# A Hymba decoder layer on one core: which modulation rows are summed in the v and z stage and which beside the xBC tiles

## The chip, the cores and the metric

The kernel runs on one core of one Trainium2 chip. The metric is device microseconds of one execution of the program; where several runs are given, their median. Engines are named as in the profile: PE is TensorE (PEld its weight loads), DVE is VectorE, ACT is ScalarE, POOL is GpSimd, SP is SyncE, which only issues DMAs here.

## The reference, cut to what matters

One sequence of 1024 tokens, width 1024, one layer:

```python
h = rmsnorm(x) * (1 + scale1) + shift1
q, k, v, z, xBC, dt = split(h @ w_in)
y_attn = rmsnorm(sliding_window_attention(q, k, v, sinks, rel_bias), attn_out_norm)
y_ssm = gated_rmsnorm(ssd_scan(silu(conv4(xBC)), dt, ...), silu(z))
x1 = x + gate1 * (concat(y_attn, y_ssm) @ w_o)
h2 = rmsnorm(x1) * (1 + scale2) + shift2
out = rmsnorm(x1 + gate2 * swiglu(h2), final_norm)
```

shift1, scale1, gate1, shift2, scale2 and gate2 are the six sections of silu(c) @ w_ada + b_ada, each of 1024 numbers, that come from the vector c of 1024 conditioning values. Attention has a window of 128, 8 query heads and a bias by relative position; everything is float32.

## The kernel before, in words

**Products.** A float32 product is made of three TensorE products in a rounded 32-bit format (`mm3`, L93): each operand is split into a high part (ACT's cast, L90) and a low part (VectorE's subtraction, `sub`, L81). A weight tile of 128x1024 is loaded by SP into `raw_ring` and split by `load_w` into `ws_ring`. `raw_ring` (L123) has three slots of 128x1024, and everything that passes through it waits for a slot to be read out.

**The six sections.** Sections 0 and 1 are computed first. Sections 2 (first gate), 3 and 4 (second norm's shift and scale) are the *rows*: `ada_row(sec, parts, kks)` (L399) loads, for each kk, one 128x1024 block of the weights through `raw_ring`, and VectorE multiplies it by one column of the conditioning and adds it to an accumulator (L407 for the first of eight, L409 for the others; `ada_rest` is `in_ada_rest` in the trace). The accumulator still has to be summed over its 128 partitions. For the gate, `gate` (L411) does it with two products against a matrix of ones (psg, L414), after its bias row has been loaded through the ring and added (L420 to L422). For the second norm, `second_mod` (L637) makes sixteen transposes into four psum banks (ps_gv, L642) and four reductions on VectorE (L643).

**Stages around the change.** The v and z projection runs over eight tiles of 128 tokens (`vz_tile`), each with two of the four psum banks of tag mm (vza and vzb). ACT frees them with a copy and two tanh, VectorE with two products (L369) and an addition. After tile 3 the bias table is built: a product, VectorE's L390, and three ACT DMAs gd (L392), gr (L394, one row copied to all partitions of a DRAM buffer, 1.5 MB) and tb (L396). Then come the gate's rows (`ada_row(2, ...)`, L419), the first three xBC weights (L423), the tiles 4 to 7 and `gate`. Next, four attention tiles `attn(t)` (L443) and the eight xBC tiles of half 0 (`xbc_tile`, L502). One attention tile is: scores (pss, L459), VectorE's bias and maximum (L463, reads tb), ACT's exponentials (L469), transposes (pst, L479), the product with v (psy, L486), VectorE's scaling (`mul`, L84), ACT's square sum, rstd over VectorE (L145), GpSimd (L146) and ACT, ACT's scaling (L492), and the four transposes of `mix_out` (psm_a, L438), whose split is one more L81. One xBC tile is 24 products psx of 128x512 and, on VectorE, three conv products (L515) and a gating one. The rows of sections 3 and 4 stand behind the xBC tiles, by the numbers of `MOD_ROWS`; `second_mod` follows them, and then the scan (`ssd_prep` with pacs, L554, and the operand w2, L564; `ssd_chunk` with seg, L581).

**What sets the order.** The program text is not the order of an engine: when the program is built, a scheduler puts each engine's instructions into a fixed order, in which psx products fill in between the steps of attention. SP's loads keep the program's order (L72). Each engine and each queue then works in order, and an instruction that has to wait holds up what stands behind it. The psum tag sm also has four banks, shared by all small products (pss, pst, psy, psm, psg, ps_gv, seg).

## Time and profile before

| | |
|---|---|
| median of 3 runs | 1148.93 us (1146.12 to 1150.82) |
| profiled execution | 1144.76 us, span 1143.0 us |
| mean granted clock of TensorE | 0.987 |
| busy in the span | PE 1105.0 (97%), PEld 912.4 (80%), DVE 842.6 (74%), ACT 517.2 (45%), POOL 244.6 (21%) |
| DMA | 197.29 MB, mean 173 GB/s |
| v and z tiles 0 to 7 on PE | end at 153.26 us |
| first xBC tiles and attention of tiles 0 to 3 | 156 to 240 us |

The times of the trace are those of one profiled execution, counted from the start of its span. Busy times are sums over instructions of an engine; PE's are modelled ends of pipelined products, so PE busy isn't PE at its peak. A row of the timeline gives start, duration, line, operation and, in brackets, how long the engine stood idle before it and what released it. The granted clock is a share of 2.4 GHz.

### The profile page before, as it was taken

How to read it: one execution, taken by the hardware profiler on the slowest of the kernel's cores; microseconds unless marked ns; L12 is line 12 of the kernel's file. 1: busy time of each engine (PE TensorE's matmuls, PEld its weight loads, DVE VectorE, ACT ScalarE, POOL GpSimd, SP SyncE). 2: the span in 40 equal slices, each digit the busy share in tenths (PEclk: the TensorE clock that was granted, in tenths of full speed). 3: DMA queues.
4: the chain of work that ended last, by engine and by line, in shares of the span. 5: the costliest groups of instructions: out<-in, count | busy, mean ns of one | idle time of the engine just before them, and what ended most of it. 6: DMA issues, size and time to landing. Idle time of an engine off the chain costs nothing. (4 is left out here: it accounts for less than half of the span.)

```text
span 1143.0 us, 15497 instructions
## 1 busy us (share of the span) xinstructions
PE 1105.0 (97%) x5376; PEld 912.4 (80%) x5376; DVE 842.6 (74%) x1490; ACT 517.2 (45%) x1007; POOL 244.6 (21%) x185
## 2 busy tenths in 40 slices
PE   7999999999999889999999999999999999999996
PEld 6788987787788668887888888888888878888875
DVE  6895368788856466546888888898788648787856
ACT  4573256756565456535443333333333325555431
POOL 0100000001200111000222124554445010451352
PEclk9999999999999969999999999999999999999998
DMA  7555644421320253236753247556764468788733
GB/s 267 189 173 174 238 151 145 137 74 38 148 75 19 102 185 119 76 127 221 249 189 125 67 148 263 194 179 217 256 201 160 157 226 306 252 292 281 234 104 147
DMA packets 80449, 197.29 MB, mean 173 GB/s; under 512 B 9154, under 2 KB 10226, under 8 KB 80244
## 3 DMA queue, kind: packets, MB, share of 16 engines
q1 hardware_dynamic: 74164, 184.95, 47.4%
q10 hardware_dynamic: 6208, 11.37, 2.8%
q8 instruction: 42, 0.69, 0.2%
q14 instruction: 35, 0.29, 0.1%
HBM read 149.87 MB, written 47.98 MB: 173 GB/s over the span
## 5 line engine op out<-in xcount | busy, mean ns | idle before, releaser
L81 DVE TENSOR_TENSOR FR<-FP,FR 128x512 fp32r<-128x512 f32 (+4 forms) x244 | 195.0, 822 | 68.8 <-ACT FR L90 68.3
L90 ACT CAST FR<-FP 128x512 fp32r<-128x512 f32 (+3 forms) x236 | 157.7, 682 | 185.6 <-PE psg L95 79.8
L797 POOL TENSOR_TENSOR GF<-GF 128x512 f32<-128x512 f32 x77 | 124.0, 1633 | 68.9 <-DMA GF<-in_w_dn 65.8
L94 PE MATMUL psg<-FR 128*128 128x512 f32 x306 | 119.0, 389 | 0.0
L95 PE MATMUL psg<-FR 128*128 128x512 f32 x306 | 119.0, 389 | 0.0
L96 PE MATMUL psg<-FR 128*128 128x512 f32 x306 | 119.0, 389 | 0.0
L146 POOL TENSOR_TENSOR FP<-FP 128x1 f32<-128x1 f32 (+1 forms) x40 | 28.3, 713 | 407.8 <-DVE FP L145 351.6
L87 DVE TENSOR_TENSOR GF<-GF,psg 128x512 f32<-128x512 f32 x126 | 84.2, 680 | 30.4 <-PE psg L96 27.9
L90 ACT CAST FR<-GF 128x512 fp32r<-128x512 f32 x77 | 47.4, 619 | 79.8 <-PE psg L95 54.5
L94 PE MATMUL psg<-GR,FR 128*128 128x512 f32 x198 | 77.0, 389 | 0.0
L95 PE MATMUL psg<-GR,FR 128*128 128x512 f32 x198 | 77.0, 389 | 0.0
L96 PE MATMUL psg<-GR,FR 128*128 128x512 f32 x198 | 77.0, 389 | 0.0
L81 DVE TENSOR_TENSOR FR<-GF,FR 128x512 fp32r<-128x512 f32 x77 | 73.1, 951 | 0.9 <-ACT FR L90 0.7
L95 PEld LDWEIGHTS psg<-FR 128*128 128x128 f32 x306 | 57.4, 188 | 12.0
L94 PEld LDWEIGHTS psg<-FR 128*128 128x128 f32 x306 | 57.4, 188 | 11.9
L96 PEld LDWEIGHTS psg<-FR 128*128 128x128 f32 x306 | 57.4, 188 | 11.9
L803 POOL TENSOR_TENSOR GD<-GD 128x512 f32<-128x512 f32 x23 | 35.7, 1562 | 119.7 <-ACT GD L415 57.7
L800 POOL TENSOR_TENSOR GF<-GF 128x512 f32<-128x512 f32 x11 | 15.5, 1405 | 194.3 <-DVE GF L84 156.2
L94 PE MATMUL psgu<-FR 128*128 128x512 f32 x128 | 51.6, 407 | 2.5 <-DVE FR L179 1.3
L94 PE MATMUL psx<-FR 128*128 128x512 f32 x128 | 52.2, 408 | 0.0
L96 PE MATMUL psgu<-FR 128*128 128x512 f32 x128 | 51.4, 403 | 0.5 <-DVE FR L81 0.5
L95 PE MATMUL psx<-FR 128*128 128x512 f32 x128 | 51.8, 405 | 0.0
(318 smaller groups left out, 2748.6 us busy)
## 6 DMA issues: line engine op xcount, KB each, us to landing
FP<-in_w_gu SPq DMA_DIRECT2D x52, 512.0 KB, 4.2
FP<-in_ada_rest SPq DMA_DIRECT2D x24, 512.0 KB, 4.4
actds<-GF SPq DMA_DIRECT2D x44, 256.0 KB, 2.7
GF<-in_w_dn SPq DMA_DIRECT2D x22, 512.0 KB, 4.6
wdndt<-GF SPq DMA_DIRECT2D x44, 256.0 KB, 4.4
FP<-actds SPq DMA_DIRECT2D x44, 256.0 KB, 4.4
FP<-wdndt SPq DMA_DIRECT2D x44, 256.0 KB, 4.4
FP<-actda SPq DMA_DIRECT2D x33, 256.0 KB, 4.2
```

The source lines that it names most:

```text
L81: nc.vector.tensor_tensor(out=out, in0=a, in1=b, op=ALU.subtract)
L87: nc.vector.tensor_tensor(out=out, in0=a, in1=b, op=ALU.add)
L90: nc.scalar.copy(h, raw)
L94: nc.tensor.matmul(ps, lhsT=lh, rhs=rh, start=first, stop=False)
L95: nc.tensor.matmul(ps, lhsT=lh, rhs=rl, start=False, stop=False)
L96: nc.tensor.matmul(ps, lhsT=ll, rhs=rh, start=False, stop=last)
L146: nc.gpsimd.tensor_tensor(out=r, in0=r, in1=mhalf[:, 0:count], op=ALU.pow)
L797: nc.gpsimd.tensor_tensor(out=out, in0=a, in1=b, op=ALU.subtract)
L800: nc.gpsimd.tensor_tensor(out=out, in0=a, in1=b, op=ALU.add)
L803: nc.gpsimd.tensor_tensor(out=out, in0=a, in1=b, op=ALU.mult)
```

## The change

The rows of sections 3 and 4 are loaded and multiplied where those of section 2 stood, and the other way round. Section 3 stands ahead of the first three xBC weights; in the text of the program two rows of section 4 follow each of the tiles 4 to 7; the transposes and reductions of the second norm stand behind tile 7, where the gate's products were. One row of the gate follows each xBC tile of half 0, and its bias row and its products stand behind the eighth. Section 3, until now accumulated as one 128x1024, becomes two parts of 128x512, as section 4 was; section 2 remains one 128x1024. Rows, transposes, reductions and gate products are the same in number.

```diff
--- before.py
+++ after.py
@@ -18,7 +18,6 @@
 KT = 8
 NF = 22
 XNB = ((0, 4, 36, 40), (0, 4, 36, 40))
-MOD_ROWS = (3, 3, 3, 3, 2, 2, 0, 0)
 NP = 11
 WARM = (16, 5)
 EPS = 1e-6
@@ -414,16 +413,23 @@
             nc.tensor.matmul(ps, lhsT=ones, rhs=a[:, 512 * e:512 * e + 512], start=True, stop=True)
             nc.scalar.copy(g[e], ps)
 
-    arow = view(FA, 16, [D])
     gate1 = [view(FA, 14, [512]), view(FA, 48, [512])]
-    ada_row(2, [arow])
-    brow = raw_ring([D])[0:1]
-    dma(brow, adab_g[0:1])
-    add(arow[0:1], arow[0:1], brow)
+    mod2 = [[view(FA, 20 + 4 * j + 2 * k, [512]) for k in range(2)] for j in range(2)]
+    ada_row(3, mod2[0])
     xw = [load_w(w_xbc[f], [KT, P]) for f in range(3)]
     for t in range(4, 8):
         vz_tile(t)
-    gate(2, gate1, arow)
+        ada_row(4, mod2[1], [2 * t - 8, 2 * t - 7])
+    sh2, g2 = M(8), M(8)
+    gv2 = M(16)
+    for j in range(4):
+        ps = sm_bank(f"ps_gv2{j}")
+        for k in range(4):
+            nc.tensor.transpose(ps[:, k * P:(k + 1) * P], mod2[j // 2][j % 2][:, k * P:(k + 1) * P], ident)
+        nc.vector.reduce_sum(out=gv2[:, 4 * j:4 * j + 4], in_=ps.rearrange("p (a b) -> p a b", a=4), axis=AX.X)
+    add(sh2, gv2[:, 0:8], pt[:, C_ADAB + 24:C_ADAB + 32])
+    mul(g2, gv2[:, 8:16], pt[:, C_N2:C_N2 + 8])
+    add(g2, g2, nb2)
 
 
     p_w.__exit__(None, None, None)
@@ -632,29 +638,16 @@
             nc.scalar.activation(y[:, 256 * g:256 * g + 256], y[:, 256 * g:256 * g + 256], AF.Copy, scale=r[:, g:g + 1])
         mix_out(y, t, 1, f"s{t}")
 
-    sh2, g2 = M(8), M(8)
-
-    def second_mod():
-        gv2 = M(16)
-        for j in range(4):
-            ps = sm_bank(f"ps_gv2{j}")
-            for k in range(4):
-                nc.tensor.transpose(ps[:, k * P:(k + 1) * P], mod2[j // 2][j % 2][:, k * P:(k + 1) * P], ident)
-            nc.vector.reduce_sum(out=gv2[:, 4 * j:4 * j + 4], in_=ps.rearrange("p (a b) -> p a b", a=4), axis=AX.X)
-        add(sh2, gv2[:, 0:8], pt[:, C_ADAB + 24:C_ADAB + 32])
-        mul(g2, gv2[:, 8:16], pt[:, C_N2:C_N2 + 8])
-        add(g2, g2, nb2)
-
-    mod2 = [[view(FB, 18, [512]), view(FB, 20, [512])], [view(FB, 22, [512]), view(FA, 46, [512])]]
     for t in range(4):
         attn(t)
-    rows = [(3 + r // 8, r % 8) for r in range(16)]
+    arow = view(FB, 18, [D])
     for f in range(8):
         xbc_tile(0, f)
-        for _ in range(MOD_ROWS[f]):
-            sec, kk = rows.pop(0)
-            ada_row(sec, [view(FB, 18, [D])] if sec == 3 else mod2[1], [kk])
-    second_mod()
+        ada_row(2, [arow], [f])
+    brow = raw_ring([D])[0:1]
+    dma(brow, adab_g[0:1])
+    add(arow[0:1], arow[0:1], brow)
+    gate(2, gate1, arow)
     prep = ssd_prep(0)
     for t in range(4):
         ssd_chunk(t, prep)
```

**Where the scheduler puts it.** The change is written as moved code, and the order of the engines moves with it. Below, FA, FB, FP and FR are SBUF tensors, names with a number are psum banks, and the lines of the changed kernel are one less than before up to its L415 (L369 is now L368, L409 L408) and six more in attention and the xBC tiles (L459 is now L465, L515 L521). On SP the bias row of the gate moves from ahead of the first three xBC weights to behind the last row, so those three weights come one place earlier.

VectorE in the v and z stage, from the first product that frees a bank of tile 3 to the first that frees one of tile 4. vza_1077 and vzb_1078 are the banks of tile 3 in both kernels; vza_1172 (before) and vza_1178 (now) is the first bank of tile 4, which tile 6 takes again. Before:

```order
L369 SCALAR_TENSOR_TENSOR FA<-FA,vza_1077 128x196
L369 SCALAR_TENSOR_TENSOR FA<-FA,vzb_1078 128x316
L87 TENSOR_TENSOR FP<-vzb_1078,FP 128x8
L390 SCALAR_TENSOR_TENSOR FA<-ps_rel,FA 8x384
L507 COPY FA<-FP 128x3
L369 SCALAR_TENSOR_TENSOR FA<-FA,vza_1172 128x196
```

Now:

```order
L406 TENSOR_SCALAR FA<-FP 128x512 x2
L408 SCALAR_TENSOR_TENSOR FA<-FP,FA 128x512
L368 SCALAR_TENSOR_TENSOR FA<-FA,vza_1077 128x196
L408 SCALAR_TENSOR_TENSOR FA<-FP,FA 128x512 x4
L368 SCALAR_TENSOR_TENSOR FA<-FA,vzb_1078 128x316
L86 TENSOR_TENSOR FP<-vzb_1078,FP 128x8
L389 SCALAR_TENSOR_TENSOR FA<-ps_rel,FA 8x384
L408 SCALAR_TENSOR_TENSOR FA<-FP,FA 128x512 x5
L513 COPY FA<-FP 128x3
L408 SCALAR_TENSOR_TENSOR FA<-FP,FA 128x512 x4
L368 SCALAR_TENSOR_TENSOR FA<-FA,vza_1178 128x196
```

The sixteen products of section 4's eight rows (L406 and L408) now stand ahead of tile 4's first product, three of them ahead of tile 3's first and seven ahead of the mask's L390 (now L389).

TensorE right behind v and z tile 7, before:

```order
L414 MATMUL psg_0_1400<-FA,FP 128x512
L414 MATMUL psg_1_1403<-FA,FP 128x512
L459 MATMUL pss_0_1412<-FA 128x128 x2
L459 MATMUL pss_1_1417<-FA 128x128 x2
L459 MATMUL pss_2_1422<-FA 128x128 x2
L459 MATMUL pss_3_1427<-FA 128x128 x2
L94 MATMUL psx_0_1736<-FR 128x512
```

Now:

```order
L428 MATMUL ps_gv_1430<-FP,FA 128x128 x4
L428 MATMUL ps_gv_1436<-FP,FA 128x128 x4
L428 MATMUL ps_gv_1442<-FP,FA 128x128 x4
L428 MATMUL ps_gv_1448<-FP,FA 128x128 x4
L465 MATMUL pss_0_1463<-FA 128x128 x2
L93 MATMUL psx_0_1787<-FR 128x512
L465 MATMUL pss_1_1468<-FA 128x128 x2
L94 MATMUL psx_0_1787<-FR 128x512
L465 MATMUL pss_2_1473<-FA 128x128 x2
L95 MATMUL psx_0_1787<-FR 128x512
```

Sixteen transposes into four banks stand where the gate's two banks were filled, and the four pss, which came one behind the other, have one psx between each other.

VectorE in attn(0), from ahead of the product that reads psy to the rstd and behind it, before:

```order
L409 SCALAR_TENSOR_TENSOR FB<-FP,FB 128x1024
L84 TENSOR_TENSOR FA<-psy_1457,FP 128x512
L510 COPY FP<-FA 128x3
L515 SCALAR_TENSOR_TENSOR FA<-FA,FP 128x512
L409 SCALAR_TENSOR_TENSOR FB<-FP,FB 128x1024
L145 TENSOR_SCALAR FP<-FP 128x1
L515 SCALAR_TENSOR_TENSOR FA<-FA,FP 128x512
L409 SCALAR_TENSOR_TENSOR FB<-FP,FB 128x1024
L515 SCALAR_TENSOR_TENSOR FA<-FA,FP 128x512
```

Now:

```order
L477 RECIPROCAL FP<-FP 128x8
L516 COPY FP<-FA 128x3
L408 SCALAR_TENSOR_TENSOR FB<-FP,FB 128x1024
L83 TENSOR_TENSOR FA<-psy_1508,FP 128x512
L521 SCALAR_TENSOR_TENSOR FA<-FA,FP 128x512
L80 TENSOR_TENSOR FR<-FP,FR 128x1024
L521 SCALAR_TENSOR_TENSOR FA<-FA,FP 128x512
L144 TENSOR_SCALAR FP<-FP 128x1
L86 TENSOR_TENSOR FB<-FB 128x32
```

Between psy's product and L145 (now L144) a row product (L409) and a conv product stood; now two conv products and a weight split (L80, the former L81) stand there. On TensorE 22, 17, 14 and 17 psx stood between the last psy product and psm_a of attn(0) to attn(3); now it is 26, 22, 18 and 16. Between pss and the first pst there were 15 and 13 in the first two tiles, and there are 18 and 15 now.

## Rows read from the trace of the kernel before

**Rows 1.** Busy time by stretch: us, PE, PEld, DVE, ACT, POOL, PEclk, DMA share, GB/s.
```profile
156.00:180.00 24.00, 22.62 (x122) 17.45 (x121) 21.64 (x68) 18.69 (x48) 0.99 (x1) 1.00 0.52 165
180.00:200.00 20.00, 18.31 (x108) 14.75 (x108) 17.86 (x48) 10.81 (x30) 0.99 (x1) 1.00 0.51 174
200.00:220.00 20.00, 18.46 (x110) 15.08 (x109) 16.07 (x48) 13.97 (x36) 1.46 (x1) 1.00 0.33 117
220.00:240.00 20.00, 19.30 (x120) 16.65 (x119) 14.89 (x28) 13.47 (x28) 1.46 (x1) 1.00 0.41 132
```

**Rows 2.** Waits of PE from 156 to 240 us: total, times, longest.
```profile
PE psm_a L438 <- ACT FA L492: 3.4, 4, 1.1
PE pst L479 <- ACT FB L469: 1.1, 2, 0.8
PE pss L459 <- DVE FR L81: 0.8, 2, 0.4
```

**Rows 3.** Timeline of DVE, attn(0): start, us, line, operation [idle before].
```profile
165.08 1.28 DVE L409 SCALAR_TENSOR_TENSOR FB<-FP,FB 128x1024 f32<-128x1024 f32 x1 [1.18 <-DMA FP<-in_ada_rest]
...
166.28 0.68 DVE L84 TENSOR_TENSOR FA<-psy,FP 128x512 f32<-128x512 f32 x1
...
167.61 1.28 DVE L409 SCALAR_TENSOR_TENSOR FB<-FP,FB 128x1024 f32<-128x1024 f32 x1
...
168.81 0.15 DVE L145 TENSOR_SCALAR FP<-FP 128x1 f32<-128x1 f32 x1
```

**Rows 4.** Timeline of PE in the same place.
```profile
169.13 0.39 PE L94 MATMUL psx<-FR 128*128 128x512 f32 x1
169.36 0.39 PE L95 MATMUL psx<-FR 128*128 128x512 f32 x1
170.83 0.66 PE L438 MATMUL psm_a<-FP,FA 128*128 128x128 f32 x4 [1.08 <-ACT FA L492]
```

**Rows 5.** DVE by line and shape, 80 to 330 us: busy, mean ns, idle before.
```profile
L81 DVE TENSOR_TENSOR FR<-FP,FR 128x1024 fp32r<-128x1024 f32 x16 | 19.4, 1216 | 4.4 <-ACT FR L90 4.4
...
L409 DVE SCALAR_TENSOR_TENSOR FA<-FP,FA 128x1024 f32<-128x1024 f32 x7 | 9.0, 1283 | 3.1 <-DMA FP<-in_ada_rest 2.8
...
L409 DVE SCALAR_TENSOR_TENSOR FB<-FP,FB 128x512 f32<-128x512 f32 x7 | 5.2, 744 | 1.5 <-DMA FP<-in_ada_rest 1.5
...
L643 DVE TENSOR_REDUCE FP<-ps_gv 128x4 f32<-128x512 f32 x4 | 2.6, 682 | 0.0
```

**Rows 6.** DMA issues (98 to 114 us, 111 to 126 us: median to landing) and SP's timeline.
```profile
FP<-in_ada_rest SPq DMA_DIRECT2D x6, 512.0 KB, 4.8
...
FP<-in_w_xbc SPq DMA_DIRECT2D x3, 512.0 KB, 5.4
...
112.39 3.24 SPq L72 DMA_DIRECT2D FP<-in_w_xbc  x3
```

**Rows 7.** Timeline of PE: v and z tile 6 begins; the gate's products.
```profile
138.99 0.32 PE L94 MATMUL vza<-FR 128*128 128x324 f32 x1
...
153.26 1.88 PE L414 MATMUL psg<-FA,FP 128*128 128x512 f32 x4
```

**Rows 8.** Mask of the bias table: DVE's row, ACT's two issues, DMA landing.
```profile
125.00 0.54 DVE L390 SCALAR_TENSOR_TENSOR FA<-ps_rel,FA 8x384 f32<-8x384 f32 x1
...
127.21 0.56 ACTq L394 DMA_DIRECT2D gr<-gd  x1
...
135.72 0.43 ACTq L396 DMA_DIRECT2D FA<-gr  x1
...
FA<-gr ACTq DMA_DIRECT2D x1, 1024.0 KB, 8.0
```

**Rows 9.** Timelines of PE and DVE behind the last xBC tile of half 0.
```profile
240.10 0.38 PE L554 MATMUL pacs<-FP,FB 128*128 128x128 f32 x2
...
248.69 1.22 DVE L84 TENSOR_TENSOR FR<-FB,FP 128x1024 fp32r<-128x1024 f32 x1
```

**Rows 10.** Busy time by stretch, second norm of half 0 (columns as in group 1).
```profile
400.00:420.00 20.00, 16.60 (x60) 12.58 (x61) 14.59 (x25) 11.50 (x17) 2.91 (x2) 0.59 0.46 172
```

## The prediction

> **What bounds the kernel now.** I read the busy times by stretch first. From 156 to 240 us, while the first four attention tiles and the xBC tiles of half 0 run, TensorE is busy 22.62, 18.31, 18.46 and 19.30 us of 84, so 5.3 us are idle there, and VectorE is nearly full in the first half of it: 21.64 of 24 us, then 17.86 of 20 [rows 1]. Second, TensorE's waits of that stretch: 3.4 us in four waits of psm_a (the transposes of the normed attention output) for ACT's L492, 1.1 us of pst for the exponentials, 0.8 us of pss for VectorE's L81 [rows 2]. They add up to the 5.3 us, so this is all that the stage can give. Third, the timelines around psm_a of attn(0), to see who is late behind ACT. VectorE stands in a row product (L409) until 166.28, 1.18 us of it waiting for the row's transfer, and only then multiplies psy; another row product of 1.28 us stands between that and the L145 that the rstd needs [rows 3]. psm_a comes at 170.83, two us after L145, and TensorE has waited 1.08 us for it [rows 4]. So the rows lengthen the chain from psy to psm_a.
>
> **What the change removes from VectorE there.** The second norm's sixteen rows were 7 products of 128x1024 at 1.28 us, 14 of 128x512 at 0.744 us [rows 5], and three first products that I count at the same prices, which is an upper bound: 8 x 1.28 + 16 x 0.744 = 22.1 us. The first gate's eight rows come instead: 8 x 1.28 = 10.3 us. VectorE loses about 12 us of 70.5 busy in the stretch [rows 1], and about half of the head-of-line waits for landings. The four reductions (0.682 us each [rows 5]) leave the end of the stretch for its beginning.
>
> **What becomes of the waits.** TensorE's order is fixed when the program is built, and it changes with the rows. Between psy and psm_a stood 22, 17, 14 and 17 psx products; now 26, 22, 18 and 16. One psx starts 0.23 us after the other [rows 4], so the covers are 6.0, 5.1, 4.1 and 3.7 us instead of 5.1, 3.9, 3.2 and 3.9. The new chain in attn(0): the psy product 0.68 us [rows 3]; then two conv products of 128x512 (the same kind and size as the 0.744 us row) and one weight split of 1.216 us [rows 5], 2.7 us; L145 0.15 us; and the 2.0 us from L145 to psm_a [rows 3, 4]. That is 5.5 us against a cover of 6.0. The wait of 1.08 us goes, with half a us to spare. In the next two tiles the cover grows by 1.2 and 0.9 us and row products leave the chain, in the last it shrinks by one psx while VectorE is freer. I leave 0.3 us of the 3.4. The cover between pss and pst grows from 15 to 18 and from 13 to 15 psx, which is 0.5 to 0.7 us against waits of at most 0.8: I leave none of the 1.1. The pss wait needs a psum bank that VectorE's split of psm_a gives back; it is not shortened, and I keep its 0.8. **Recovered: 5.3 - 1.1 = 4.2 us.** The ends: 5.3 if all go, 1.1 if only pst's go.
>
> **What it adds to the v and z stage.** Section 3's rows take the gate's place ahead of the weights; eight more, section 4's, run beside tiles 3 and 4, where VectorE's own work is light, but it works in order, and the two psum banks of tile 4 are freed by products (L369) that now stand behind all eight rows. Tile 6 takes these banks at 138.99 [rows 7]. When are the rows done? The raw ring has three slots. The first weight load behind the rows of section 3 is issued at 112.39 now; it moves one ring slot forward, because the bias row leaves the ring, so I take about 111.5, plus 5.4 us to landing [rows 6], plus a split of about 2.3 us (ACT's cast and the 1.216 us of rows 5): the first row's load goes out near 119, the next two near 121 and 122. A slot then turns round in 4.8 us of landing [rows 6], 1.5 us for two products and 0.3 us of handing over, 6.6 us. Row 6 is issued near 132, row 7 near 134: the last product ends at 138.5 to 140.5. Tile 6 waits nothing to 2 us; I take **+0.8 us**. The upper bound comes from the gr copy below, the slowest load of this place: at its 8.5 us for the last two rows they end near 143, and tile 6 waits 4 us.
>
> Behind these rows on VectorE stands the mask's product (L390), now at 125.00; four and a half us later it starts the gd, gr and tb copies on ACT's queue. gr is issued at 127.21 and has landed by 135.72, when tb is issued; tb takes 8.0 us [rows 8]. Moved to 132, that makes 140.5 and 149, ahead of the first bias product, by my estimate near 157 (the stretch of attn(0) starts at 156): nothing, though 8 us of slack are left where there were 12. ACT's next copy, of tile 5's bank, stands behind tb's issue on its queue, some 4 us ahead of tile 7, which takes that bank: nothing.
>
> **Behind the v and z stage** sixteen transposes take the place of the gate's products, 1.88 us [rows 7]. psm_a's four transposes of the same size take 0.66 us together [rows 4], so sixteen take some 2.6 us at most, and less back to back; the same exchange the other way round stands behind the xBC tiles, so the two cancel. But they use all four small psum banks, and pss can begin in each only when its reduction is done. The reductions start when VectorE has finished tile 7, by my estimate a little over 1 us behind tile 7's end at 153.26, and follow each other every 0.68 us [rows 5, 7]; TensorE would be there some 2 us behind that end and now has a psx between the pss. I take **+0.4 us**; the ends are nothing and 2.7 us, four reductions in a row.
>
> **Behind the xBC tiles** the gate's products stand where the transposes stood; their rows were complete two tiles earlier, so they wait for none. Without the reductions the seg products move nearer to pacs: 25 psx behind it, 5.7 us, where pacs is at 240.10 and the operand's product (L84) runs from 248.69 [rows 9], 44 psx behind. VectorE has to do one split, three conv products and that one in between, 1.2 + 2.2 + 1.2 us and small ones; it is nearly even. I take **+0.4 us**, from nothing to 1. DMA traffic, ACT's work, SP's number of loads (24 rows, one bias row) and the order behind the second norm are the same; the out projection has long had its gate. GpSimd's work is the same too.
>
> **Sum.** -4.2 + 0.8 + 0.4 + 0.4 = -2.6 us. The profiled execution took 1144.76 us, so 1142.2; it lies 4.2 us under the median of the three runs, 1148.93, and against that the forecast is **1146.3 us**. From 1143.2 to 1154.7, 0.5% either way, a measurement of this kernel can't tell it from no change.
>
> **Rivals.** *The waits stay where they are.* psm_a waits for ACT and GpSimd, and the conv products and splits that are left on VectorE fill the place of the rows: the chain of attn(0) came out only 0.5 us under its cover. If it is 0.5 to 1 us longer in each tile, only pst's 1.1 us come back, and with the 1.6 us added the time is 1149.4. For it: rstd's way over three engines is not touched. Against it: in the second and third tile the cover grows by more than the chain.
>
> *The rows jam the v and z stage* (the slower side). The rows' transfers fall together with the 1.5 MB gr copy, which now starts later, beside the last rows. If each of these takes gr's 8.5 us, tile 6 waits 4 us; gr itself, at twice its 8.5 us, lands at 149, so ACT stands at tb's issue until then, frees tile 5's bank 3 us after tile 7 wants it near 146, halfway between the two rows of TensorE [rows 7], and tb lands at 157, just as the bias products ask for it. Counted 4 + 1 + 0.5 us beyond what is saved or hidden, against 4.2 - 0.8 us of gain, the time is about 1151; if the attention waits stay too, 1155. It decides from a row landing above about 6 us. In the trace one row beside gr landed in less than the 4.8 us of the others, which speaks against it. The Trainium skill (DMA: Bandwidth & Descriptors, Queues, rings and completion order) says that each DMA engine takes the queues it has work for in turn, packet by packet, so that loads of SP and copies of ACT share it. By that rule gr is drawn out by the rows for as long as rows are waiting, which is this rival's price; no run here shows the two with more than three rows.
>
> *The half-clock stretch moves.* From 400 to 420 us the granted clock is 0.59 of 2.4 GHz, so most of it is at 1.2 GHz, with 16.60 us of work [rows 10], behind the wait of the second norm's transposes for VectorE. At 2.4 GHz the work would have taken 0.59 of that, 6.8 us less. The order there is unchanged, but everything arrives earlier; if the stretch were shorter by two thirds, the time is about 1142, and a longer one costs as much as 3 us. Nothing in the change speaks for either.
>
> **How the numbers follow.** The forecast has 0.55, the staying waits 0.22, the jam 0.12, a shorter clock stretch 0.11. Faster by over 0.5% needs all 5.3 us and more, or the clock: 0.10 from the last rival and 0.07 from the forecast's edge, 0.17. Slower by over 0.5% is the worse half of the jam, 0.06, and 0.02 for what I overlook, 0.08. The rest, 0.75, is no change. The bounds of the forecast's own terms reach from 1143.6 (5.3 recovered, nothing added) to 1151 (1.1 and half of the upper bounds); the range takes in most of the clock rival at its lower end and the milder jam at its upper: 1141.5 to 1151.5.
>
> **What would show it.** Right: VectorE's busy time from 156 to 200 us falls by 8 us or more, psm_a's four waits by 2.5 us or more, the vza products of tile 6 wait under 2 us, pss waits under 1 us behind the v and z stage, and the first xBC tile of half 1 begins 2 to 4 us earlier. Wrong: psm_a still waits 3 us in all; a wait of vza above 3 us for L369; tb landing behind the first bias product; a stretch of 1.2 GHz in the v and z stage, or none near 400 us.

## The result, and the profile after

Eight runs of the changed kernel took 1155.69 us in the median (1151.26 to 1163.61), eight of the kernel before 1148.57 us (1145.71 to 1151.1): a ratio of 1.0073, with a 95% interval of 1.0053 to 1.0092. The change makes the kernel slower by 0.7%. The forecast was 1146.3 us, no change, with a range of 1141.5 to 1151.5. The profiled execution took 1155.87 us, its span 1154.1 us; the mean granted clock is 0.983 (0.987 before), PE is busy for 1111.4 us, DVE for 841.5. A *hole* below is time in which TensorE stands idle ahead of a product.

Busy time by stretch in the changed kernel, the columns and stretches of [rows 1]:

```profile
156.00:180.00 24.00, 23.21 (x109) 18.13 (x108) 16.52 (x51) 11.60 (x33) 1.20 (x1) 0.86 0.41 131
180.00:200.00 20.00, 19.73 (x115) 16.28 (x115) 16.14 (x50) 14.55 (x36) 1.46 (x1) 1.00 0.20 68
200.00:220.00 20.00, 19.79 (x115) 16.06 (x113) 16.60 (x46) 14.44 (x34) 1.54 (x1) 1.00 0.22 80
220.00:240.00 20.00, 18.19 (x108) 15.08 (x108) 13.61 (x39) 13.32 (x33) 1.69 (x2) 1.00 0.30 106
```

TensorE idles 3.1 us of the 84 where it idled 5.3, and VectorE has lost 7.6 us. But in the first stretch the granted clock is 0.86: TensorE is busy because its products take longer. Waits of PE from 156 to 242.5 us, to be held against [rows 2]:

```profile
PE psm_a L444 <- ACT FA L498: 2.4, 2, 1.5
PE pss L465 <- DVE FP L429: 0.8, 1, 0.8
PE pss L465 <- DVE FR L80: 0.7, 2, 0.4
```

Of psm_a's 3.4 us 2.4 are left, pst's 1.1 us are gone, and the scores have a new wait of 0.8 us for the reductions (L429). TensorE's timeline from v and z tile 6 to the second xBC products ([rows 7] before):

```profile
141.03 0.41 PE L93 MATMUL vza<-FR 128*128 128x324 f32 x1 [2.05 <-DVE FA L368]
...
155.39 1.91 PE L428 MATMUL ps_gv<-FP,FA 128*128 128x128 f32 x16
158.09 0.71 PE L465 MATMUL pss<-FA 64*128 64x128 f32 x4 [0.79 <-DVE FP L429]
158.73 0.50 PE L93 MATMUL psx<-FR 128*128 128x512 f32 x1
159.16 0.71 PE L465 MATMUL pss<-FA 64*128 64x128 f32 x4
159.80 0.56 PE L94 MATMUL psx<-FR 128*128 128x512 f32 x1
160.28 1.22 PE L465 MATMUL pss<-FA 64*128 64x128 f32 x4
161.44 0.79 PE L95 MATMUL psx<-FR 128*128 128x512 f32 x1
162.16 1.22 PE L465 MATMUL pss<-FA 64*128 64x128 f32 x4
```

Four things stand there that the kernel before doesn't have: 2.05 us of waiting ahead of tile 6, 0.79 us ahead of the scores, scores pulled apart by single psx, and from 160 us on everything at half speed (four scores 1.22 us where they took 0.71). The clock by stretch says the same:

```profile
158.00:162.00 4.00, 3.91 (x15) 2.62 (x15) 3.60 (x18) 0.00 (x0) 0.00 (x0) 0.76 0.40 136
162.00:166.00 4.00, 4.00 (x11) 3.08 (x11) 2.76 (x11) 1.18 (x7) 0.00 (x0) 0.50 0.05 8
```

In the kernel before, the scores of attn(0) ran as one block:

```profile
155.06 1.46 PE L459 MATMUL pss<-FA 64*128 64x128 f32 x16
156.45 0.50 PE L94 MATMUL psx<-FR 128*128 128x512 f32 x1
```

Sixteen records in 1.39 us there, four in 0.64 us here (each of the eight float32 score products leaves two records). Why the wait of the scores: the rows hold VectorE's mask product (L390, now L389), and that holds three ACT copies. DVE, then ACT's queue, in the changed kernel ([rows 8] before):

```profile
130.66 0.53 DVE L389 SCALAR_TENSOR_TENSOR FA<-ps_rel,FA 8x384 f32<-8x384 f32 x1
```

```profile
135.00 0.56 ACTq L393 DMA_DIRECT2D gr<-gd  x1
...
145.57 0.42 ACTq L395 DMA_DIRECT2D FA<-gr  x1
146.04 0.27 ACT L362 COPY FA<-vza 128x128 f32<-128x128 f32 x1 [9.77 <-DMA gr<-gd]
...
155.60 0.33 ACTq L622 DMA_DIRECT2D FA<-gzd  x1
155.97 0.27 ACT L362 COPY FA<-vza 128x128 f32<-128x128 f32 x1 [7.03 <-DMA gzd<-FA]
```

gr is issued 7.8 us later than before and takes 10.5 us to land where it took 8.5; ACT stands idle until 145.57, then frees tile 5's bank and stores two tiles shortly after each other; at 155.60 it issues the scan's first reload of the gated z (L622), which had to wait for one of these stores, and only then frees tile 7's banks, 6 us later than before. The reductions come behind that.

How much of this is the clock can be counted over all runs, since each lists its mean granted clock. I call (1 - clock) x time the *clock loss* and clock x time the *rest*. Means: before 1131.1 + 16.3 us (35 runs, beside the first experiments), changed 1136.1 + 20.1 us (8 runs). So the change costs 5.0 us of rest and 3.8 us of clock (standard errors near 0.8 and 1.4 us). The eight runs of the kernel before that stand beside the changed ones have no clock on record; their mean is 1148.4 us, 1.0 us above those 35, so up to 1 us of these 8.8 can be a difference between the two sets of runs.

### The profile page after: what moved, and what is told of

Its sections match the earlier page's. It is cut to its first block, busy times and chain, and to the rows that moved or that the text cites. A ratio compares the mean times of both kernels' runs of the same rounds, so it can differ in the third digit from the quotient of the medians.

```text
span 1154.1 us, 15514 instructions
## 1 busy us (share of the span) xinstructions
PE 1111.4 (96%) x5376; PEld 918.3 (80%) x5376; DVE 841.5 (73%) x1498; ACT 515.7 (45%) x1007; POOL 249.2 (22%) x185
## 5 line engine op out<-in xcount | busy, mean ns | idle before, releaser
L80 DVE TENSOR_TENSOR FR<-FP,FR 128x512 fp32r<-128x512 f32 (+4 forms) x244 | 196.7, 827 | 68.7 <-ACT FR L89 64.7
L145 POOL TENSOR_TENSOR FP<-FP 128x1 f32<-128x1 f32 (+1 forms) x40 | 30.9, 779 | 421.2 <-DVE FP L144 361.8
L86 DVE TENSOR_TENSOR GF<-GF,psg 128x512 f32<-128x512 f32 x126 | 84.3, 680 | 28.4 <-PE psg L95 26.9
L80 DVE TENSOR_TENSOR FR<-GF,FR 128x512 fp32r<-128x512 f32 x77 | 71.2, 927 | 1.5 <-ACT FR L89 1.4
L93 PE MATMUL psgu<-FR 128*128 128x512 f32 x128 | 51.3, 404 | 2.4 <-DVE FR L178 1.2
L94 PE MATMUL psx<-FR 128*128 128x512 f32 x128 | 53.5, 418 | 0.0
L95 PE MATMUL psx<-FR 128*128 128x512 f32 x128 | 53.4, 417 | 0.0
L93 PE MATMUL psx<-FR 128*128 128x512 f32 x128 | 53.0, 414 | 0.0
```

What stands on the lines that cost most here:

```text
L80: nc.vector.tensor_tensor(out=out, in0=a, in1=b, op=ALU.subtract)
L86: nc.vector.tensor_tensor(out=out, in0=a, in1=b, op=ALU.add)
L93: nc.tensor.matmul(ps, lhsT=lh, rhs=rh, start=first, stop=False)
L94: nc.tensor.matmul(ps, lhsT=lh, rhs=rl, start=False, stop=False)
L95: nc.tensor.matmul(ps, lhsT=ll, rhs=rh, start=False, stop=last)
L145: nc.gpsimd.tensor_tensor(out=r, in0=r, in1=mhalf[:, 0:count], op=ALU.pow)
```

## Experiments on the end of the v and z stage

Theories: **A**, the block behind tile 7 (transposes in all four banks, the waiting and pulled-apart scores) costs and brings the clock down; **B**, the clock falls because of the hole ahead of tile 6. Four kernels, on one chip.

**Sums later.** The transposes and reductions behind the xBC tiles:

```diff
-    mod2 = [[view(FA, 20 + 4 * j + 2 * k, [512]) for k in range(2)] for j in range(2)]
+    mod2 = [[view(FA, 14, [512]), view(FA, 48, [512])], [view(FA, 50, [512]), view(FA, 46, [512])]]
...
         ada_row(2, [arow], [f])
+    sh2, g2 = M(8), M(8)
+    for j in range(4):
...
```

> The changed kernel, with the second norm's sixteen transposes and four reductions moved from behind v and z tile 7 to behind the xBC tiles, ahead of the gate's bias; the four sums wait in FA 14, 48, 50 and 46, and the mask's table moves to FA 30. Rows and loads stay as changed. Theory A (what costs is the block behind tile 7: the wait of the scores for the reductions, the scores' products pulled apart by single psx, and the clock that falls to 1.2 GHz right behind them): the four pss stand together again (16 products in about 1.4 us), no wait of 0.8 us, no fall of the clock near 160 us, so 5 to 6 us less than the changed kernel, a ratio to before of 1.002 (1.000 to 1.004). Theory B (the clock falls because of the 2 us hole ahead of tile 6): the fall near 160 stays, only some 2 us are saved, ratio 1.005 to 1.006.

Measured: 1.0024 (1.0002 to 1.0045). The scores stand together. In the profiled execution the hole ahead of tile 6 was longer, and the clock fell right behind it, at 143 us:

```profile
141.88 0.41 PE L93 MATMUL vza<-FR 128*128 128x324 f32 x1 [3.25 <-DVE FA L368]
```

```profile
144.00:148.00 4.00, 4.00 (x22) 4.00 (x21) 0.74 (x4) 0.50 (x2) 0.00 (x0) 0.69 0.96 329
```

**VectorE's order pinned**, so that two rows of section 4 come behind each tile's products:

```diff
-        vz_tile(t)
-        ada_row(4, mod2[1], [2 * t - 8, 2 * t - 7])
+        ada_row(4, mod2[1], [2 * t - 8, 2 * t - 7], tc.keep_in_program_order)
+        vz_tile(t)
```

> The changed kernel, with VectorE's order pinned in the v and z stage: the row products of section 4 may not stand ahead of the products that free the banks of tile 3, 4, 5 or 6 (two rows behind each). TensorE's order and everything behind the stage stay as changed. Theory A: the 2.05 us wait of tile 6 goes, the block behind tile 7 still waits, is pulled apart and lets the clock fall: 2 us less than the changed kernel, ratio to before 1.0055 (1.004 to 1.007). Theory B: the fall near 160 us goes with the hole of tile 6: 5 us less, ratio 1.003.

Measured: 1.0038 (1.0019 to 1.0057). No hole ahead of tile 6 and none ahead of the scores, since ACT and VectorE are earlier too; no fall of the clock. The scores are as pulled apart as before, now all at full clock:

```profile
154.45 1.91 PE L428 MATMUL ps_gv<-FP,FA 128*128 128x128 f32 x16
156.38 0.71 PE L465 MATMUL pss<-FA 64*128 64x128 f32 x4
157.02 0.51 PE L93 MATMUL psx<-FR 128*128 128x512 f32 x1
...
159.59 0.71 PE L465 MATMUL pss<-FA 64*128 64x128 f32 x4
160.23 0.51 PE L93 MATMUL psx<-FR 128*128 128x512 f32 x1
```

From the first score to the psx behind the last, 3.85 us with three psx in between; the kernel before needs 1.39 us and three psx at some 0.25 us each. So the pulling apart costs 1.7 us by itself, which was in no term of the forecast.

**Small products.** The column sums in one bank, without reductions:

```diff
-    for j in range(4):
-        ps = sm_bank(f"ps_gv2{j}")
-        for k in range(4):
-            nc.tensor.transpose(ps[:, k * P:(k + 1) * P], mod2[j // 2][j % 2][:, k * P:(k + 1) * P], ident)
-        nc.vector.reduce_sum(out=gv2[:, 4 * j:4 * j + 4], in_=ps.rearrange("p (a b) -> p a b", a=4), axis=AX.X)
+    ps = sm_bank("ps_gv2")
+    for i in range(16):
+        nc.tensor.matmul(ps[:, i:i + 1], lhsT=mod2[i // 8][i // 4 % 2][:, i % 4 * P:(i % 4 + 1) * P], rhs=ones[:, 0:1], start=True, stop=True)
+    gv2 = ps[:, 0:16]
```

> The changed kernel, with the sixteen transposes and four reductions replaced, in the same place, by sixteen products of 128x1 against a column of ones, all in one psum bank, which VectorE reads without a reduction. Theory A: three banks stay free, the pss stand together and wait for nothing, so as in the late kernel 5 to 6 us less than the changed kernel, ratio 1.002 (1.000 to 1.004). If instead the many small products themselves let the clock fall, it falls near 160 us here too and the ratio is 1.005 or more. Theory B: as the late kernel, 1.005 to 1.006.

Measured: 0.9998 (0.9977 to 1.0019), some 9 us less than the changed kernel. In TensorE's timeline the small products take 1.6 us more than the transposes, and the clock falls for a short stretch behind them, but the scores stand together and wait for nothing.

**Sums later and order pinned.**

> Both edits: the transposes and reductions behind the xBC tiles, and VectorE's order pinned in the v and z stage. Theory A: the two costs add, 7 to 8 us less than the changed kernel, ratio 1.000 (0.997 to 1.002). Theory B: with the hole of tile 6 gone the clock stays up, and the ratio is the same 1.000, so this run tells the theories apart only with the other two. Rival C (the loss sits in the second half, where attention waits 1.6 us more than before, and in more falls of the clock at 300 to 430 us): neither edit reaches it, ratio 1.004 or more in all four.

Measured: 1.0024 (1.0006 to 1.0041).

What follows: by the means of all runs, in us against the changed kernel, sums later give 1.6 of rest and 4.4 of clock, the pin 1.7 and 3.0, both 3.0 and 3.5, the small products 6.8 and 2.1 (standard errors near 0.9 and 1.5). So either edit gives some 1.6 us of its own, and the clock loss is lower where either is made; A and B each hold in part. That the clock loss needs both places is an argument and not shown. For it: three kernels further down that leave both places as they are have 19.2, 20.0 and 20.4 us of clock loss. Against it: a fourth such kernel, without GpSimd's power, has 17.0; and these are means over whole executions, which don't say where the clock was lost. The profiles do, for one execution each. From tile 4 to the second norm the kernel before and the three experiments on it lost none, in five profiles; the changed kernel lost 5.1 and 6.8 us, sums later 3.4, the pin none, both 1.7. And 1.7 us in each of nine of the fifteen profiles with moved rows are another fall, between 276 and 300 us in the scan, in the kernel with both edits too; what brings it is open.

The hole ahead of tile 6 differs between executions. Seven profiled executions have the changed kernel's order on TensorE, VectorE and ACT up to tile 6: the changed kernel twice, sums later, the small products, and three that follow (without the power, without the gate's rows, reloads on SP). In them it is 2.05, 1.60, 3.25, 0.44, 1.13, 0 and 0 us, 1.2 in the mean. It goes with the landing of section 4's last row: 8.8 us in sums later, where it fell together with gr, 6.0 in the changed kernel, 4.5 and 4.8 in the two without a hole.

Nor do these edits change one thing alone, since the scheduler moved psx products in attention with them. The covers of the first half are 26, 22, 18 and 16 psx in the changed kernel, 19, 18, 17 and 17 with the small products and with sums later. With the small products psm_a waits 0.9 us less in the first half and 1.1 less in the second, and the scan's transposes (psm_s) 1.1 less, so some 3 of the 6.8 us are not those of the block behind tile 7. The rest of the kernel with both edits is still 2.0 us above the kernel before in the mean; in its profile the time from tile 4 to the second norm, at full clock, is 1.1 to 1.4 us shorter than in the kernel before's two, so what is left does not show in this stretch.

## Experiments on the attention stage

Theory **R** is the forecast's (the row products on VectorE set psm_a's waits), theory **G** puts them on the hop over GpSimd between VectorE's L145 (L144 in the changed kernel) and ACT's scaling. By the *chain* of a tile I mean the time from the end of psy to psm_a, by its *cover* the psx that TensorE has in between. What led to G is GpSimd's power in the first half's four tiles, changed kernel:

```profile
177.38 1.20 POOL L145 TENSOR_TENSOR FP<-FP 128x1 f32<-128x1 f32 x1 [136.71 <-DVE FP L144]
198.33 1.46 POOL L145 TENSOR_TENSOR FP<-FP 128x1 f32<-128x1 f32 x1 [19.75 <-DVE FP L144]
218.46 2.13 POOL L145 TENSOR_TENSOR FP<-FP 128x1 f32<-128x1 f32 x1 [18.67 <-DVE FP L144]
238.90 1.46 POOL L145 TENSOR_TENSOR FP<-FP 128x1 f32<-128x1 f32 x1 [18.32 <-DVE FP L144]
```

and the kernel before:

```profile
169.03 0.99 POOL L146 TENSOR_TENSOR FP<-FP 128x1 f32<-128x1 f32 x1 [128.42 <-DVE FP L145]
188.34 0.99 POOL L146 TENSOR_TENSOR FP<-FP 128x1 f32<-128x1 f32 x1 [18.32 <-DVE FP L145]
208.22 1.46 POOL L146 TENSOR_TENSOR FP<-FP 128x1 f32<-128x1 f32 x1 [18.89 <-DVE FP L145]
228.45 1.46 POOL L146 TENSOR_TENSOR FP<-FP 128x1 f32<-128x1 f32 x1 [18.76 <-DVE FP L145]
```

One number for each partition takes up to 2.13 us, and longer with fewer rows on VectorE; in the second half of the kernel before, where VectorE is less full, it takes 0.55 us in all four tiles. In 218.46 to 220.59 VectorE runs conv products and a weight split without a gap. What decides is whether VectorE is in the middle of an instruction when the power starts. The 18 profiles that have the power show 145 of 128x1 between 150 and 392 us. The 55 that begin beside no VectorE instruction of over 0.3 us all take 0.55 to 0.56 us. Of the 90 that begin during one, 74 end 0.4 to 0.5 us behind its end, nine last longer (2.1 to 2.8 us), and seven take 0.55.

> The kernel before, without GpSimd's power -0.5 in the norms of the attention and scan outputs (16 tiles): VectorE's L145 gives a constant near 1 in its place, so those two norms are left out; every other instruction, the rows beside the xBC tiles among them, stays. Theory G (psm_a waits for the hop over GpSimd, whose 128x1 power takes 0.55 us where VectorE is free and 1 to 2.1 us where VectorE streams from SBUF, and not for the row products): three of the four psm_a waits go though all rows are still there, and so do psm_s's 2 us; only attn(0)'s 1.08 us, where row products stand ahead of psy's product, may stay in part. 4 to 5 us less, ratio 0.996. Theory R (the row products on VectorE set the waits, as the prediction had it): psm_a's 3.4 us fall by at most the direct hop, some 0.5 us each, and 1.5 to 2 us are won in all, ratio 0.998.

Edit, in `rstd_of`, for the names of attention and scan: `tensor_scalar(out=r, in0=ss, scalar1=1e-9, scalar2=1.0, ...)` and no power. Measured: 0.9937 (0.9918 to 0.9957), 7.2 us less. All rows are still there, the covers are those of the kernel before but for one psx, and psm_a waits for nothing:

```profile
PE pst L482 <- ACT FB L472: 1.7, 2, 0.9
PE pss L462 <- DVE FR L81: 0.4, 1, 0.4
```

> The changed kernel with the same power left out in the same 16 tiles. Theory G: psm_a's 2.4 us and 1.1 us in the two halves and psm_s's 2.8 us go, 5 to 6 us less than the changed kernel, ratio to before 1.002; what stays is tile 6's 2 us, the block behind tile 7 and the falls of the clock. Theory R: the rows are gone from the chain already, so the waits that are left have another cause, ratio 1.005 or more.

Measured: 0.9970 (0.9946 to 0.9994), 12 us less than the changed kernel; psm_a's waits are gone in both halves under unchanged covers (26, 22, 18 and 16 psx), the two holes at the v and z stage stay (1.1 and 2.3 us in its profile) and the clock falls behind them.

> The kernel before without the sixteen rows of the second norm (their four accumulators are set to zero, so the second norm's modulation is left out); transposes and reductions stay. Theory R: no row stands in any chain of attention, the 5.3 us of waits shrink to 1 us or less, ratio 0.996. Theory G: only attn(0)'s 1.08 us and part of pst's 1.1 us go, the other three psm_a waits stay at 0.5 to 1.1 us each because conv products and splits stand where the rows stood and hold GpSimd as well; ratio 0.998 to 1.000.

Edit: the inner loop over `MOD_ROWS` taken out, two `memset` over the four accumulators. Measured: 0.9981 (0.9966 to 0.9997), 2.2 us less. The waits of the first half fall to

```profile
PE psm_a L438 <- ACT FA L492: 0.9, 2, 0.7
```

which looks nearer to R than to G, but it doesn't decide. The longest of the waits, 1.12 us in attn(2), fell to 0.20 because its cover grew from 14 to 18 psx; its chain stayed at 4.4 us. In attn(3) chain and cover both shrank a little, and its 0.70 us became 0.68. The power takes 0.55 us in three tiles of four here.

> The changed kernel without the gate's eight rows beside the xBC tiles (the accumulator is set to zero, so the first gate is left out but for its bias). Theory G (the hop over GpSimd sets the waits that are left): the conv products and splits still stretch its power, so of psm_a's 2.4 us in the first half 1 us or more stays, and the kernel is no more than 2 us faster than the changed one, ratio to before 1.005. Theory R (row products set them): psm_a's waits of the first half go, 2.5 us less or more, ratio 1.004.

Measured: 1.0039 (1.0014 to 1.0064), 4 us less than the changed kernel; psm_a still waits 1.6 us in the first half and nothing in the second, though no row at all stands beside the xBC tiles. In attn(2) the chain is 1.0 us shorter than in the changed kernel, but the cover is two psx shorter, and 0.94 us of wait stay.

> The kernel with the small products and the pinned order, and in the norms of attention and scan ACT does VectorE's mean-plus-epsilon of 128x1 (one 0.2 us activation right behind its own square sum), so that the chain goes ACT, GpSimd, ACT and no longer queues on VectorE. Theory G: the chain from psy to psm_a becomes 0.3 to 1 us shorter in each of the eight attention tiles, what is left is GpSimd's power; psm_a's 1.5 us fall to under 1 and psm_s's 1.4 us too: 1 to 2 us less than without it, ratio 0.996 to 0.997. Against it: ACT's own queue then has 16 activations more, 3 us in all. If the ratio is 0.998 or more, VectorE's queue was not what the chain stood in.

Edit: in `rstd_of`, `nc.scalar.activation(r, ss, AF.Identity, scale=1.0 / n, bias=...)` for L145 in attention and scan. Measured: 1.0024 (1.0009 to 1.0039), 5 us slower than without it. The chain grew to 5.3 to 5.6 us in three of four tiles, psm_a waits 2.8 us. Moving L145 from VectorE's queue to ACT's gained nothing; what VectorE's queue had cost the run doesn't tell, since the psx in between have moved too.

What follows: the wait of psm_a is what a chain over four engines has beyond its cover. Taking out the power alone brings the chain below the cover in every tile of both kernels, with the covers nearly or wholly unchanged; that is shown. Taking out all rows leaves 0.9 of 3.4 us in the kernel before and 1.6 of 2.4 in the changed one; there the scheduler moved the covers with the rows, so what the rows alone are worth is not shown. The Trainium skill (SBUF — State Buffer, SBUF: two separate sides) says that VectorE and GpSimd share a pair of ports, and that a VectorE operation with two inputs in SBUF holds it for its whole instruction against a GpSimd operation that reads SBUF. The durations above agree: 0.55 us alone, and an end shortly behind that of the VectorE instruction beside conv products, splits and rows, all of which have two such inputs. That a power can wait for a second such instruction too (2.13 us, where the longest of the three lasts 1.21) is from the rows alone.

## Experiments on ACT's lateness, and a better version

**Both v and z edits that won most:** small products and the pinned order.

> The changed kernel with both edits that touch the v and z stage and its end: VectorE's order pinned there, and the column sums of the second norm as sixteen products of 128x1 in one bank. Theory A with the stage clean: no hole ahead of tile 6 (in the kernel with the ones alone it was 0.4 us), no wait of the scores, so 1 to 3 us less than that kernel: ratio 0.998 (0.996 to 1.000), and no fall of the clock between 140 and 175 us. If the small products bring the clock down by themselves, it falls behind them as in that kernel (at 159 us) and the ratio is 1.000.

Measured: 0.9976 (0.9960 to 0.9992), faster than both kernels. No hole from tile 4 to the end of psm_a's first tile, attention's second half waits 0.3 us; the small products bring the clock down for a short time behind them, as in the kernel with them alone:

```profile
154.53 3.63 PE L426 MATMUL ps_gv<-FP,FA 128*128 128x1 f32 x32
158.09 2.07 PE L463 MATMUL pss<-FA 64*128 64x128 f32 x16
```

```profile
158.00:162.00 4.00, 4.00 (x23) 3.43 (x23) 3.60 (x22) 0.00 (x0) 0.00 (x0) 0.57 0.19 68
```

**Second profiles** of the two kernels, one run each:

> The kernel before, unchanged, for a second profile: how much of a stage's difference between two profiles is no more than two executions of one program. The stretch from the first product of the second norm (ps_h of half 0) to the end took 727 us at full clock in its first profile and 728 to 732 us in those of the other kernels, though all have the same order there. If the change alone made that, it is 727 again; if it is chance, it is 729 to 731.

> The changed kernel, unchanged, for a second profile. Theory A and B together (the fall of the clock behind the v and z stage needs the hole ahead of tile 6 and the pulled-apart block behind tile 7): a wait of 1 to 3 us ahead of tile 6, the scores' wait of 0.5 us or more, and a stretch of 1.2 GHz between 158 and 172 us again. If the fall was chance: none there.

The kernel before repeated every step from tile 4 to the second norm within 0.4 us, but took 2.6 us more ahead of tile 4 and 5.6 us more from the first ps_h to TensorE's last product, 733 against 727 (both at full clock, that is, less the clock loss): the first profile was a lucky one there, and no difference of a few us between two profiles in those parts says anything of the change. The changed kernel repeated its holes (1.6 us and 2.2 us) and its fall:

```profile
156.00:160.00 4.00, 1.79 (x15) 1.41 (x13) 2.25 (x7) 1.06 (x4) 0.00 (x0) 0.97 0.34 125
160.00:170.00 10.00, 10.00 (x26) 7.06 (x26) 7.25 (x29) 2.78 (x15) 0.00 (x0) 0.50 0.29 84
```

**The mask two tiles earlier** (its block between tiles 1 and 2 of the program), on the changed kernel, on the better version and on the kernel before:

> The changed kernel, with the bias mask's block (its three small loads, its product, VectorE's mask product and the gd, gr and tb copies) moved two v and z tiles earlier, between tiles 1 and 2. TensorE's order behind tile 7 is unchanged: sixteen transposes, then the scores with single psx between. Theory M (the late mask chain on ACT's queue makes the reductions late): gr is issued near 113 us, ACT is free when tile 7's banks are full, the scores wait 0.3 us or less, no fall of the clock between 155 and 175 us, tile 6 waits under 1 us: 4 to 7 us less than the changed kernel, ratio to before 1.002 (1.000 to 1.004). Theory A' (the block of transposes and pulled-apart scores lets the clock fall by itself): the fall is still there, ratio 1.005 or more.

> The kernel with the small products and the pinned order (ratio 0.9976), with the mask's block two tiles earlier as well. Theory M: its v and z stage has no hole left to close, so little is won: ratio 0.996 to 0.998. If the small products behind tile 7 still bring the clock down for one short stretch near 159 us, that is their own doing and not ACT's lateness.

> The kernel before with the mask's block two tiles earlier, as a control. Nothing waits for the mask in the kernel before (tb lands some 12 us ahead of the first score), so no theory expects a change: ratio 1.000 (0.998 to 1.002). If it is faster by 0.3% or more, the earlier mask gains something of its own and the two other runs must be read against it.

Measured: 1.0121 (1.0101 to 1.0141), 1.0002 (0.9984 to 1.0020) and 1.0004 (0.9993 to 1.0015). The control is as expected. On the changed kernel the edit did the opposite of what the theory said: gr now lands beside the weights and the first rows, which VectorE waits for,

```profile
126.98 0.88 DVE L408 TENSOR_SCALAR FA<-FP 128x512 f32<-128x512 f32 x2 [8.47 <-DMA FP<-in_ada_rest]
```

ACT stands at tb's issue until 128.65 us, the lateness goes on from tile to tile to the same reload (at 159.13 us), the scores wait 3.5 us and the clock falls. So the chain is the one described, longer. What stands ahead of it, by these landings, is that the rows and the 1.5 MB copy slow each other wherever they meet.

**The first two reloads of the gated z on SP**, so that ACT doesn't stand at them; no other instruction changes its place:

```diff
-        nc.scalar.dma_start(gz, gz_d[t])
+        if t < 2:
+            dma(gz, gz_d[t])
+        else:
+            nc.scalar.dma_start(gz, gz_d[t])
```

> The changed kernel, with the first two reloads of the gated z (chunks 0 and 1 of the scan) issued by SP, behind the gate's bias row, instead of by ACT; no other instruction changes its order on any engine. Theory L (ACT stands at the first reload until the store of tile 6 has landed, so tile 7's tanh, VectorE's products and the reductions come late): ACT frees tile 7's banks as soon as they are full, the scores wait 0.3 us or less instead of 0.8 to 2.2, the clock does not fall between 155 and 175 us; the wait of tile 6 and the pulled-apart scores stay. 4 to 6 us less than the changed kernel, ratio to before 1.003 (1.001 to 1.004). Theory A' (the block itself lets the clock fall): ratio 1.006 or more, with a fall near 160 us.

> The kernel with the small products and the pinned order (ratio 0.9976), with the first two reloads on SP. There ACT's late release holds nobody, since the small products take 3.55 us and the scores find their banks free: ratio 0.998 (0.996 to 0.999), no difference that can be told.

> The changed kernel with the pinned order and the first two reloads on SP. Theory L: no hole ahead of tile 6 and none ahead of the scores, no fall of the clock there; what is left of the loss is the pulled-apart scores, 1 to 2 us, and the second half's 1.6 us, against 2 us won in the first half: ratio 1.002 (1.000 to 1.004).

Measured: 1.0069 (1.0050 to 1.0088), 0.9974 (0.9959 to 0.9989) and 1.0045 (1.0028 to 1.0062). On the changed kernel this was a miss: the profiled run has neither hole nor fall at the v and z stage, but the clock loss over its six runs is 20.0 us, as in the changed kernel. The reload explains the 0.8 to 2.2 us that the profiles show ahead of the scores; the kernel without the gate's rows has 1.5 us there with no hole ahead of tile 6, so the two holes don't need each other. It doesn't explain the clock; where the other five runs lost theirs no profile shows. With the pin it changes nothing that can be told.

## Why the prediction was wrong, step by step

- **"So the rows lengthen the chain from psy to psm_a", "the 2.0 us from L145 to psm_a", and so "Recovered: 5.3 - 1.1 = 4.2 us".** This step failed first: I read attn(0) and took it for all four tiles. In attn(2) and attn(3), which have 1.8 of psm_a's 3.4 us, no row product stood between psy and L145 in the kernel before; this is attn(2):

```profile
206.13 0.69 DVE L84 TENSOR_TENSOR FA<-psy,FP 128x512 f32<-128x512 f32 x1 [0.56 <-PE psy L486]
206.74 0.68 DVE L518 SCALAR_TENSOR_TENSOR FA<-FA 128x512 f32<-128x512 f32 x1
207.34 0.74 DVE L515 SCALAR_TENSOR_TENSOR FA<-FA,FP 128x512 f32<-128x512 f32 x1
208.00 0.14 DVE L145 TENSOR_SCALAR FP<-FP 128x1 f32<-128x1 f32 x1
```

  And from L145 to psm_a it is 2.0, 2.0, 2.5 and 2.5 us there, 2.7, 2.8, 3.1 and 2.5 in the changed kernel, because GpSimd's power in the middle takes 1.2 to 2.1 us beside VectorE's streaming. In attn(2) the change even brought a new instruction into the chain, which no term held: the addition of the gate's bias row (L86, on one partition), 1.21 us.

```profile
217.11 1.21 DVE L86 TENSOR_TENSOR FB<-FB,FP 1x1024 f32<-1x1024 f32 x1
218.25 0.13 DVE L144 TENSOR_SCALAR FP<-FP 128x1 f32<-128x1 f32 x1
```

```profile
221.40 0.66 PE L444 MATMUL psm_a<-FP,FA 128*128 128x128 f32 x4 [1.49 <-ACT FA L498]
```

  The cover there grew to 18 psx, 4.1 us, as counted, but the chain grew from 4.40 to 5.66 us, half of it ahead of L144 and half behind. With 0.93 us in attn(3), 2.4 us of wait stayed where I left 0.3. Right were VectorE's rows (11.2 us less by the profiles, 12 in the sum), and attn(0), attn(1) and pst, whose waits went; the pst covers of 15 and 13 psx, put down to the first two tiles ahead of the forecast, are those of attn(1) and attn(2), where the waits stood. In all 2.2 us came back, less 0.8 for the scores.
- **"Tile 6 waits nothing to 2 us; +0.8".** The mechanism, its place and, over the seven profiles of this order, its size were right: 0 to 3.25 us, 1.2 in the mean. The two of the changed kernel itself, 2.05 and 1.6, lie at the upper end of the forecast's. In the first of them the last row ended at 140.7, 0.2 us past the late end of the sum.
- **"Behind the v and z stage +0.4", the ends 0 and 2.7.** 0.8 and 2.2 us of wait, within the ends; but the reductions were late for ACT's reload, which the text had not seen (it had gr issued at 132 and landed at 140.5; that came at 135.0 and 145.5, and the stores and the reload behind it), and that "a psx between the pss" is a price of its own, 1.7 us, was not in the sum.
- **The clock.** The text named a stretch of 1.2 GHz at the v and z stage only as something that would prove it wrong. The clock cost 3.8 us in the mean, as far as the two sets of runs can be held against each other. What the profiles show: near the v and z stage the clock fell to 1.2 GHz behind a hole of 1.5 us or more in six, and behind or during the small products, without a hole of over 0.5 us, in all five that have them. Which idle time or which products decide, and why the mean loss stayed at 20.0 us with the reloads on SP, is open.
- **"The order behind the second norm is the same"** is true, but attention's second half stands ahead of it, and its order moved as well: it waited for nothing before, and now

```profile
PE psm_a L444 <- ACT FA L498: 1.1, 4, 0.3
PE pst L485 <- ACT FB L475: 0.3, 1, 0.3
```

  with 0.2 us of pss, 1.6 us that no term held.
- **The rivals.** The jam was the nearest, in mechanism and in its time of 1151 to 1155: the rows issued from 111 to 126 us landed in 6.1 us (median), those from 126 to 146 in 4.1, the last row that tile 6 needs in 6.0, and gr in 10.5. So its condition was met at the edge. That its time is so near is in part luck: it had tile 5's bank freed 3 us late, which cost nothing, put 4 us on tile 6, and had neither the reload, nor the pulled-apart scores, nor the clock. Its chance of 0.12 was too low for a case whose condition lay 1.2 us from a measured 4.8. The staying waits were half true.

By the first profiles, to the second norm: 2.2 us at tile 6, 0.9 us up to the scores, 1.7 us of pulled-apart scores, 1.6 us in the second half, 5.1 us of clock (3.4 behind the v and z stage, 1.7 at 297 us in the scan), less 2.2 us: 9.3 us, where ps_h of half 0 starts 8.5 us later. Of the mean rest of 5.0 us, this holds 3.4 to 4.2; the remainder isn't placed. Whether the small products would gain the same in the kernel before was not tried.

## What to carry to other kernels

A chain over several engines is costed in each tile with what will stand beside it, not by the tile that one has looked at: take work off one engine, and the scheduler puts other work there, which can stretch the chain and hold its next engine as long. A wait that was read in one tile is looked for in the others before it is multiplied. A hole that depends on when a transfer lands differs from one execution of the same order to the next (0 to 3.25 us here), so one profile doesn't give its size. Count what an edit does to adjacency as well: sums that take all banks of a shared tag pulled the scores apart, and a column sum as products against ones in a single bank, with VectorE's order pinned behind the bank-freeing products, turned 0.7% lost into 0.2% won, though that edit moved attention's order as well. A move of late loads past a copy on another queue moves everything that queue holds, down to the reload of a ring slot.

## What the runs showed of the hardware that I had not expected

- Score products of 64x128, in groups that use the two halves of the array's rows by turns (`rows` in `attn`): sixteen records in a row take 1.39 us, 0.09 us each; with a psx on both sides four take 0.64 us, 0.16 each. I read that as two groups running at once; a price of each change between them and the 128-row psx would look the same, and no run took it apart.
- A power of 128x1 on GpSimd takes 0.55 us where VectorE isn't in the middle of an instruction (all 55 of 55), and ends 0.4 to 0.5 us behind the VectorE instruction that it began in (74 of 90), which made up to 2.13 us of it in this change.
- Sixteen float32 products of 128x1 (32 records) took 3.6 us, sixteen transposes of 128x128 1.9 us, and behind or during the small ones the clock fell in five profiles of five, with no hole of over 0.5 us.
- Two executions of one program differ, at full clock, by 2.6 us ahead of tile 4 and by 5.6 us behind the first ps_h of the second norm, while 271 us in between repeat within 0.4 us.
